# Up projection in Strassen-Winograd form: where the low parts of two halo columns are multiplied

## The chip, the cores and the metric

The kernel runs on one core of a Trainium2 chip (one of the eight; the others are idle). The metric is the device time of one execution in microseconds. Times are medians of several executions of the same program; a profiled execution gives the trace.

## The reference, cut to what matters

One layer of a hybrid decoder: a mixer (attention and a convolution module) with a residual layer norm, and a convolutional feed-forward part. Only the latter is touched here:

```python
h = layer_norm(DEEPNORM_ALPHA * h + mixed @ w_out, ln1_g, ln1_b)   # (1, 1040, 1024) float32
up = causal_dwconv(h @ ffn_w_up, ffn_dw, ffn_dw_b)                 # ffn_w_up (1024, 5632), 3 taps over the sequence
u, g = jnp.split(up, 2, axis=-1)
f = (jax.nn.gelu(g, approximate=False) * u) @ ffn_w_down           # ffn_w_down (2816, 1024)
return layer_norm(DEEPNORM_ALPHA * h + f, ln2_g, ln2_b)
```

The result is float32. The causal convolution over three positions needs, for each half of the sequence (512 positions), the two positions ahead of it: the halo, so 514 columns in all.

## The kernel before, in words

**Three products for one.** TensorE works on a reduced float32 type (`R`, float32r). To keep float32's precision each operand x is split into a high part (its copy in `R`, by ScalarE) and a low part (x minus the high part, by VectorE), and a product is the sum of three matmuls in one accumulation: high x high, high x low, low x high.

**The up projection** (lines 1446 to 1582) is a two by two block product with seven sub-products (Strassen-Winograd): the sequence is one block index (two halves), the 1024 input features the other of the right operand, and a turn `c` (22 of them) makes the 128 channels of the u half and of the gate half that belong together. Its seven right operands B11, B21, BT2, BT4, BT1, BT3, B22 are formed once (`form_t2` and its like, `bsplit`) and stay in SBUF; the seven left operands (weights) are formed and split in each turn by `wsplit`, up to nine ahead of their use. `prod` issues one sub-product: for each of four blocks `k` of 128 features three matmuls. Its columns are cut into two (`SUB`): sub 0 has 258 columns (two of halo and 256), sub 1 has 256. So a sub-product has 24 matmuls, a turn 7 x 24 = 168, and the whole projection 22 x 168 = 3696.

The right operands of sub 0 lie in blocks of `BS[0]` = 260 columns, four high blocks and then four low ones, and the last two columns of a block are unused; those of sub 1 lie in blocks of 256. `bsum(sub, q, hl)` gives the four blocks of the high (`hl` 0) or low part, `bmat` one of them.

**PSUM.** Four tiles of two banks each (`V4, X, Z, Y`, 1024 columns) take the sub-products: sub 0 writes columns 254 to 511, at the end of the first bank, sub 1 columns 512 to 767, at the start of the second, so that one instruction over 514 columns reads both (`at`). Two sub-products accumulate on an earlier one's result in X and one in Y. ScalarE copies X (u13, u2, u13 again) and Y (c22) to SBUF, and VectorE forms the four results c11, c22, c21, c12 of 514 columns (`tt`, line 1542).

**After them** comes `conv_ffn` for each of the four: an activation on ScalarE (line 1461) makes the last tap with the bias, two multiply-adds on VectorE (1462, 1463) the other taps; then gelu on ScalarE (1467), a product on VectorE (1471) and a store to `fd` by SyncE's queue.

**Order of the work.** The instructions of an engine run in the order that a planner gives them when the kernel is built. It goes by priorities (`rank`) and by its own estimate of times; `after` fixes pairs by hand, and `line` chains a row of VectorE instructions, among them the splits of the right operands. Turn 0 has two passes: first sub 1 with all seven products, during which the rest of sub 0's operands is formed (`LATE`, `split_of`), then sub 0. The operands B11 and B21 of sub 0 are formed in two parts, `EARLY` (columns 0 to 129) and `LATE` (130 to 257).

**The down projection** (lines 1588 to 1763) follows. Its first operands are loaded, split and multiplied while the last turn's convolutions still run; it reads `fd`, so its loads stand in SyncE's queue behind the last stores.

Of the kernel before, what the change touches and what calls it, by code (L numbers as in the profile page):

```python
# [25 lines left out]
AF = mybir.ActivationFunctionType  # L26
OP = mybir.AluOpType
# [31 lines left out]

HW = 514  # L60
SUB = [(0, 258), (258, HW)]

WS = 144

BS = [260, 256]
# [47 lines left out]
def tile_hybrid_layer(  # L113
# [3 lines left out]
    nc = tc.nc  # L117
# [12 lines left out]
    def f32(ap):  # L130
        return ap.bitcast(F)
# [24 lines left out]
    FA = arena.tile([P, 6144], F, name="FA")  # L156
# [23 lines left out]
    start = ExitStack()  # L180
# [345 lines left out]
    first = [weights([P, KC, P], in_cols(m)) for m in (4, 5, 0)]  # L526
# [163 lines left out]
    bias = ap.tile([P, NH, 272], F, name="bias")  # L690
# [49 lines left out]
    ins = load(vd, dram(v1d, 0, [[0, P], [J_LEN, NH], [1, J_LEN]]))  # L740
# [17 lines left out]
    for g in range(NKV):  # L758
# [3 lines left out]
        for lo in (0, 64):  # L762
            for o, i in ((Kx[g][lo:, :, 16:144], kr[lo:, 16:T].rearrange("p (n c) -> p n c", c=P)),
                         (Kx[g][lo:, :, 0:16], kr[lo:, 0:16].unsqueeze(1).to_broadcast([P - lo, NB, 16]))):
                if lo == 0:
                    ins = nc.vector.tensor_copy(o, i)
                else:
                    ins = nc.vector.tensor_tensor(o, i, f32(o), OP.subtract)
# [8 lines left out]
    src = ps[:64, :P].rearrange("p (g d) -> p g d", d=HD)  # L777
    nc.scalar.copy(vm[:64, :, 0], src)
    nc.vector.tensor_tensor(vm[:64, :, 1], src, f32(vm[:64, :, 0]), OP.subtract)
    for q4 in range(2):  # L780
# [4 lines left out]
        src = ps[:, :].rearrange("p (n g d) -> p n g d", g=2, d=HD)  # L785
        for g in range(NKV):
            hi, lo = (V[:, q4 * 4:q4 * 4 + 4, g, i] for i in range(2))
# [22 lines left out]
    for h in range(NH):  # L810
        g, r = divmod(h, 4)
        o = ps[:2, h * 16:(h + 1) * 16]
        ins = nc.tensor.matmul(o, q0[g][0][:, r, 0:2], Kx[g][:, 0, 0:16], start=True, stop=False)
# [66 lines left out]
    for i in range(NB):  # L880
# [5 lines left out]
        for g in range(NKV):  # L886
            qh, ql = load_q(g, i) if i else (t[:, :, 2:] for t in q0[g])
            s = ap.tile([P, 4, 272], F, name="s", tag="s", bufs=3)
# [189 lines left out]
    RT = OB[:, 0:2048]  # L1078
# [118 lines left out]
    def bsum(sub, q, hl):  # L1197
        n, s = SUB[sub][1] - SUB[sub][0], BS[sub]
        t, o = B_AT[sub][q]
        return t[:, o + hl * 4 * s:o + (hl + 1) * 4 * s].rearrange("p (k n) -> p k n", k=4)[:, :, :n]  # L1200

    def bmat(sub, q, hl, k):
        return bsum(sub, q, hl)[:, k]

    lined, high = [], []

    def line(ins):

        if lined:
            after(ins, lined[-1])  # L1210
        lined.append(ins)
        return ins
# [3 lines left out]
    def wide(x):  # L1216
        return x.rearrange("p (k n) -> p k n", k=4)
# [3 lines left out]

    def bsplit(sub, q, src, cs=slice(None)):
        with rank(RK_SUMS):
            hi, lo = (bsum(sub, q, hl)[:, :, cs] for hl in range(2))
            src = wide(src)[:, :, cs]
            ins = nc.scalar.copy(hi, src)
            if (sub, q) in ((0, BT2), (0, BT4), (0, BT1), (0, BT3)):
                if high:
                    after(ins, high[-1])
                high.append(ins)  # L1230
            line(nc.vector.tensor_tensor(lo, src, f32(hi), OP.subtract))

    def bsub(out, x, y, cs=slice(None)):
        with rank(RK_SUMS):
# [216 lines left out]
    def ftmp():  # L1451
        i = ft_next[0] % 8
        ft_next[0] += 1
        return FA[:, i * 512:(i + 1) * 512]

    c11, c21, u2 = (FA[:, 4128 + i * HW:4128 + (i + 1) * HW] for i in range(3))
    c12, c22, u13 = (RT[:, i * HW:(i + 1) * HW] for i in range(3))

    def conv_ffn(cc, o):
        t = ftmp()  # L1460
        nc.scalar.activation(t, cc[:, 2:HW], AF.Identity, bias=ffw(3, o), scale=ffw(2, o))  # L1461
        nc.vector.scalar_tensor_tensor(t, cc[:, 1:HW - 1], ffw(1, o), t, OP.mult, OP.add)
        nc.vector.scalar_tensor_tensor(t, cc[:, 0:HW - 2], ffw(0, o), t, OP.mult, OP.add)
        return t
# [47 lines left out]
    for c in range(FC):  # L1512
        V4, X, Z, Y = (pup.tile([P, 1024], F, name=n, tag=n) for n in ("pw", "px", "pz", "py"))
        passes = ((1,), (0,)) if c == 0 else ((0, 1),)
        for subs in passes:
            last = subs == passes[-1]
            w_next = iter(range(7))
            a, b = SUB[subs[0]][0], SUB[subs[-1]][1]

            def at(t):  # L1520
                return t[:, 254 + a:254 + b]

            def prod(q, bank, first):
                if last:
                    w_ahead(9)
                    ah, al = w_ready.pop(0)
                else:
                    ah, al = w_ready[next(w_next)]
                for sub in subs:
                    o = bank[:, 254 + SUB[sub][0]:254 + SUB[sub][1]]  # L1530
                    for k in range(4):
                        ks = slice(k * P, (k + 1) * P)
                        for j, (x, hl) in enumerate(((ah, 0), (ah, 1), (al, 0))):
                            ins = nc.tensor.matmul(o, x[:, ks], bmat(sub, q, hl, k), start=first and k + j == 0,  # L1534
                                                   stop=k == 3 and j == 2, skip_group_check=not first)
                            if k + j == 0 and last_mm:
                                after(ins, last_mm[-1])
                    last_mm.append(ins)

            def tt(*x):  # L1540
                with rank(RK_CHAIN):
                    return nc.vector.tensor_tensor(*x)  # L1542

            def copy(*x):
                with rank(RK_CHAIN):
                    copied.append(nc.scalar.copy(*x))  # L1546

            prod(B11, X, True)
            copy(u13[:, a:b], at(X))
            prod(B21, Z, True)  # L1550
            if last and c not in (0, FH + 1):
                sums_load(c - 1 if c <= FH else c - 2)
            tt(c11[:, a:b], at(Z), u13[:, a:b], OP.add)
            prod(BT2, X, False)
            copy(u2[:, a:b], at(X))
            if not last:
                turn(5, *last_rows, (V4, Z), last_mm, True)
                for q in (B11, B21):
                    split_of(0, q, LATE)
                form_t2(0, LATE)  # L1560
                formed.append(lined[-1])
                form_t4(0, LATE)
                form_t3(0, LATE)
                for q in (BT2, BT4, BT1, BT3, B22):
                    split_of(0, q)
            if last:
                g0 = gelu(conv_ffn(c11, FC + c))
            prod(BT4, V4, True)
            prod(BT1, Y, True)
            copy(c22[:, a:b], at(Y))  # L1570
            prod(BT3, X, False)
            copy(u13[:, a:b], at(X))
            ins = tt(c22[:, a:b], c22[:, a:b], u13[:, a:b], OP.add)
            if last and c not in (0, FH + 1):
                sums_form(c - 1 if c <= FH else c - 2, ins)
            tt(c21[:, a:b], u13[:, a:b], at(V4), OP.subtract)
            prod(B22, Y, False)
            tt(c12[:, a:b], at(Y), u2[:, a:b], OP.add)
            if last:
                f1 = conv_ffn(c22, c)  # L1580
                f_out(c, 0, g0, conv_ffn(c21, c))
                f_out(c, 1, gelu(conv_ffn(c12, FC + c)), f1)
# [234 lines left out]
```

## Time and profile before

| | |
|---|---|
| median of 3 runs | 1271.38 us (1269.64 to 1272.08) |
| the profiled execution | 1271.08 us, span 1269.3 us |
| mean granted clock of TensorE | 0.995 |
| up projection, turn 0 | 609.00 to 633.85 us of the span |
| up projection, turns 1 to 21 | 633.85 to 1047.40 us |
| down projection and the end | 1047.40 to 1269.3 us |

The profile shows one execution. A page gives the busy time of each engine, the span in slices, the chain of work that ended last, and groups of equal instructions. PE is TensorE, DVE VectorE, ACT ScalarE, SP SyncE. In the timeline each row is one instruction or several equal ones in a row (x12): start, time until the last one ends, engine, source line, operation, `out<-in` by the program's names, tile shape. Matmuls overlap, so the time of one says little; the distance of two rows' starts, divided by the count, says how fast they follow each other.

### The profile page before, as it was taken

The numbers are of one execution on the slowest core, as the hardware profiler recorded it, in microseconds if no ns is written. First come the engines' busy times: TensorE is split into PE (matmuls) and PEld (weight loads), VectorE is DVE, ScalarE is ACT, GpSimd is POOL, SyncE is SP. The second block draws the span as 40 slices with busy tenths as digits, with TensorE's granted clock in tenths as the row PEclk, the third lists the DMA queues.
The fourth block names the chain that finished last, engine by engine and source line by source line (L and its number), as shares of the span: only waits on it lengthen the run. The fifth ranks groups of instructions, "written<-read, shape, count | busy, mean of one in ns | idle before, by whom it ended". The sixth has DMA issues, their size and how long they took to land.

```text
span 1269.3 us, 23031 instructions
## 1 busy us (share of the span) xinstructions
PE 1252.8 (99%) x9186; PEld 1184.5 (93%) x9186; DVE 1073.1 (85%) x1854; ACT 591.6 (47%) x1095; POOL 8.1 (1%) x9
## 2 busy tenths in 40 slices
PE   8999999999999999999999999999999999999997
PEld 7999999999999999788899999999999997788886
DVE  7888999999978577548999999998989975987697
ACT  7532355655473223335655455555554553535330
POOL 0000000001000000000000000000000000000000
PEclk9999999999999999999999999999999999999999
DMA  6375643332438364222245546454454566989712
GB/s 252 105 250 149 176 112 96 105 92 83 125 85 226 106 177 125 83 85 82 67 158 198 193 170 212 160 207 150 159 191 170 197 239 242 394 280 369 266 67 83
DMA packets 98701, 212.19 MB, mean 167 GB/s; under 512 B 11411, under 2 KB 38611, under 8 KB 98338
## 3 DMA queue, kind: packets, MB, share of 16 engines
q1 hardware_dynamic: 84474, 199.64, 47.3%
q10 hardware_dynamic: 14120, 11.08, 2.8%
q8 instruction: 72, 1.18, 0.4%
q14 instruction: 35, 0.29, 0.1%
HBM read 150.29 MB, written 62.70 MB: 168 GB/s over the span
## 4 chain that ended last, share of the span: by engine, by line
PE 93%; DVE 2%; DMA 2%; ACT 2%; issue 1%; SPq 0%; DVEq 0%; ACTq 0%
PE px L1534 14%; PE py L1534 10%; PE ps_x L1663 9%; PE ps_z L338 8%; PE ps_z L342 8%; PE ps_z L341 8%; PE pw L1534 5%; PE pz L1534 5%; PE ps_z L1663 5%; PE ps_p L342 2%; PE ps_p L338 2%; PE ps_p L341 2%; PE ps_w L342 2%; PE ps_w L338 2%; PE ps_w L341 2%; PE ps_z L556 2%
## 5 line engine op out<-in xcount | busy, mean ns | idle before, releaser
L342 PE MATMUL ps_z<-RHC,w 128*128 128x256 f32 (+2 forms) x864 | 244.6, 283 | 0.0
L338 PE MATMUL ps_z<-RHO,w 128*128 128x256 f32 (+2 forms) x864 | 244.4, 283 | 0.2 <-ACT FA L734 0.2
L341 PE MATMUL ps_z<-RHO,w 128*128 128x256 f32 (+2 forms) x864 | 243.2, 282 | 0.0
L338 PEld LDWEIGHTS ps_z<-RHO,w 128*128 128x128 f32 x864 | 162.6, 188 | 2.0 <-ACT FA L705 0.7
L341 PEld LDWEIGHTS ps_z<-RHO,w 128*128 128x128 f32 x864 | 162.7, 188 | 0.7
L342 PEld LDWEIGHTS ps_z<-RHC,w 128*128 128x128 f32 x864 | 162.7, 188 | 0.4
L725 DVE SCALAR_TENSOR_TENSOR FA<-cin,cdw,FA 128x1026 f32<-128x1026 f32 x120 | 152.3, 1279 | 0.7
L1356 DVE TENSOR_TENSOR RHO<-wr,RHO 128x512 fp32r<-128x512 f32 x94 | 63.5, 683 | 8.3 <-ACT RHO L1355 8.3
L1355 ACT CAST RHO<-wr 128x512 fp32r<-128x512 f32 x94 | 56.6, 619 | 23.2 <-DVE wr L1373 11.3
L300 ACT CAST w<-wr 128x1024 fp32r<-128x1024 f32 x37 | 38.7, 1046 | 60.8 <-PE ps_z L342 44.8
L734 ACT ACTIVATE FA<-ps_z,colr 128x258 f32<-128x258 f32 (+1 forms) x64 | 30.1, 472 | 69.8 <-PE ps_z L342 57.3
L1373 DVE TENSOR_TENSOR wr<-wr 128x512 f32<-128x512 f32 x88 | 60.0, 682 | 0.1
L303 DVE TENSOR_TENSOR w<-wr,w 128x1024 fp32r<-128x1024 f32 x37 | 45.0, 1217 | 16.3 <-ACT w L300 16.1
L1546 ACT COPY FA<-px 128x514 f32<-128x514 f32 (+2 forms) x23 | 13.1, 571 | 76.7 <-PE px L1534 76.7
L1356 DVE TENSOR_TENSOR w<-wr,w 128x512 fp32r<-128x512 f32 x60 | 40.6, 684 | 4.8 <-ACT w L1355 4.7
L1534 PE MATMUL px<-OA,RHO 128*128 128x258 f32 x324 | 43.2, 283 | 0.0
L1461 ACT ACTIVATE FA<-OB,coll 128x512 f32<-128x512 f32 x44 | 35.9, 815 | 15.0 <-DVE OB L1542 15.0
L1546 ACT COPY OB<-px 128x514 f32<-128x514 f32 (+2 forms) x46 | 26.2, 569 | 34.7 <-PE px L1534 34.5
L1534 PE MATMUL px<-RHC,RHO 128*128 128x258 f32 (+1 forms) x312 | 41.1, 281 | 0.4 <-ACT OB L1546 0.4
L1534 PE MATMUL px<-OC,RHO 128*128 128x256 f32 x324 | 41.5, 277 | 0.0
L1355 ACT CAST w<-wr 128x512 fp32r<-128x512 f32 x60 | 36.3, 618 | 11.1 <-DVE wr L1373 5.1
L1534 PEld LDWEIGHTS px<-OA,RHO 128*128 128x128 f32 x324 | 40.5, 189 | 0.2 <-ACT OB L1546 0.2
(442 smaller groups left out, 3297.2 us busy)
## 6 DMA issues: line engine op xcount, KB each, us to landing
wr<-in_w_up_dram SPq DMA_DIRECT2D x44, 512.0 KB, 3.6
wr<-in_w_z_dram SPq DMA_DIRECT2D x29, 512.0 KB, 3.7
fd<-FA SPq DMA_DIRECT2D x44, 256.0 KB, 2.1
OB<-in_w_down_dram SPq DMA_DIRECT2D x21, 512.0 KB, 4.8
FA<-sd SPq DMA_DIRECT2D x15, 512.0 KB, 9.0
qt<-qd SPq DMA_DIRECT2D x28, 256.0 KB, 4.1
sgd<-FA ACTq DMA_DIRECT2D x48, 128.0 KB, 2.7
td<-OB SPq DMA_DIRECT2D x12, 512.0 KB, 2.7
```

What stands on the lines that cost most here:

```text
L300: ins = nc.scalar.copy(hi, raw)
L303: return nc.vector.tensor_tensor(lo, raw, f32(hi), OP.subtract)
L338: ins = nc.tensor.matmul(ps, al, bh, start=i == 0, stop=False)
L341: nc.tensor.matmul(ps, ah, bh, start=False, stop=False)
L342: last = nc.tensor.matmul(ps, ah, bl, start=False, stop=i == n - 1)
L725: nc.vector.scalar_tensor_tensor(acc[c], cin[:, j:j + U], wc, acc[c], OP.mult, OP.add)
L1355: nc.scalar.copy(hi, src)
L1356: ins = nc.vector.tensor_tensor(lo, src, f32(hi), OP.subtract)
L1373: ins = nc.vector.tensor_tensor(*x)
L1534: ins = nc.tensor.matmul(o, x[:, ks], bmat(sub, q, hl, k), start=first and k + j == 0, stop=k == 3 and j == 2, skip_group_check=not first)
L1546: copied.append(nc.scalar.copy(*x))
L1663: nc.tensor.matmul(banks[i], l[:, ts], r[:, ws], start=first and a and x + k == 0, stop=z and x == len(ops) - 1 and k == 2, skip_group_che ...
```

## The change

In sub 0 the three matmuls of each `k` get different widths. The two halo columns of the low part are stored just before the high part, in columns 0 and 1 of each 260-column block (the high part moves to columns 2 to 259), and the low block keeps only its 256 other columns. Then:

- high weights x [halo low | high], 260 columns, into PSUM columns 252 to 511;
- high weights x low, 256 columns, into 256 to 511;
- low weights x high, 258 columns, into 254 to 511.

The halo's low product so lands in its own two PSUM columns, 252 and 253, beside the halo's other two products in 254 and 255. All copies and sums after it are 516 columns wide and carry both. In `conv_ffn` two activations on ScalarE, of one column each, add column 0 to column 2 and column 1 to column 3. When an operand is split, the halo's low part is a second, small subtraction on VectorE (seven in all, once per operand). Sub 1 is as before, and so are all other stages.

```diff
+CU = HW + 2
...
     def bsum(sub, q, hl):
         n, s = SUB[sub][1] - SUB[sub][0], BS[sub]
         t, o = B_AT[sub][q]
-        return t[:, o + hl * 4 * s:o + (hl + 1) * 4 * s].rearrange("p (k n) -> p k n", k=4)[:, :, :n]
-
-    def bmat(sub, q, hl, k):
-        return bsum(sub, q, hl)[:, k]
+        x = 2 if sub == 0 and hl == 0 else 0
+        v = t[:, o + hl * 4 * s:o + (hl + 1) * 4 * s].rearrange("p (k n) -> p k n", k=4)
+        return v[:, :, x:x + (256 if hl else n)]
+
+    def halo_low(q):
+        t, o = B_AT[0][q]
+        return t[:, o:o + 4 * BS[0]].rearrange("p (k n) -> p k n", k=4)[:, :, 0:2]
+
+    def bmat(sub, q, j, k):
+
+        if sub == 0 and j == 0:
+            t, o = B_AT[0][q]
+            return t[:, o + k * BS[0]:o + (k + 1) * BS[0]]
+        return bsum(sub, q, j % 2)[:, k]
...
     def bsplit(sub, q, src, cs=slice(None)):
         with rank(RK_SUMS):
-            hi, lo = (bsum(sub, q, hl)[:, :, cs] for hl in range(2))
             src = wide(src)[:, :, cs]
+            hi = bsum(sub, q, 0)[:, :, cs]
             ins = nc.scalar.copy(hi, src)
...
-            line(nc.vector.tensor_tensor(lo, src, f32(hi), OP.subtract))
+            n = src.shape[2]
+            first = cs.start or 0
+            x = 2 if sub == 0 and first == 0 else 0
+            at = first - 2 if sub == 0 and first else 0
+            lo = bsum(sub, q, 1)[:, :, at:at + n - x]
+            line(nc.vector.tensor_tensor(lo, src[:, :, x:], f32(hi)[:, :, x:], OP.subtract))
+            if x:
+                line(nc.vector.tensor_tensor(halo_low(q), src[:, :, :2], f32(hi)[:, :, :2], OP.subtract))
...
-    c11, c21, u2 = (FA[:, 4128 + i * HW:4128 + (i + 1) * HW] for i in range(3))
-    c12, c22, u13 = (RT[:, i * HW:(i + 1) * HW] for i in range(3))
+    c11, c21, u2 = (FA[:, 4128 + i * CU:4128 + (i + 1) * CU] for i in range(3))
+    c12, c22, u13 = (RT[:, i * CU:(i + 1) * CU] for i in range(3))
 
     def conv_ffn(cc, o):
         t = ftmp()
+        for i in range(2):
+            nc.scalar.activation(cc[:, 2 + i:3 + i], cc[:, 2 + i:3 + i], AF.Identity, bias=cc[:, i:i + 1], scale=1.0)
+        cc = cc[:, 2:]
         nc.scalar.activation(t, cc[:, 2:HW], AF.Identity, bias=ffw(3, o), scale=ffw(2, o))
...
-            a, b = SUB[subs[0]][0], SUB[subs[-1]][1]
+            a, b = SUB[subs[0]][0] + (2 if subs[0] else 0), SUB[subs[-1]][1] + 2
 
             def at(t):
-                return t[:, 254 + a:254 + b]
+                return t[:, 252 + a:252 + b]
...
                 for sub in subs:
-                    o = bank[:, 254 + SUB[sub][0]:254 + SUB[sub][1]]
                     for k in range(4):
                         ks = slice(k * P, (k + 1) * P)
-                        for j, (x, hl) in enumerate(((ah, 0), (ah, 1), (al, 0))):
-                            ins = nc.tensor.matmul(o, x[:, ks], bmat(sub, q, hl, k), start=first and k + j == 0,
+                        for j, x in enumerate((ah, ah, al)):
+                            o = bank[:, 512:768] if sub else bank[:, (252, 256, 254)[j]:512]
+                            ins = nc.tensor.matmul(o, x[:, ks], bmat(sub, q, j, k), start=first and k + j == 0,
                                                    stop=k == 3 and j == 2, skip_group_check=not first)
```

## The prediction

> **What bounds the kernel now.** I read the page's busy times first, then the chain that ended last, then the busy time by stretch over the up projection, and last the timeline of TensorE inside it.
>
> ```profile
> span 1269.3 us, 23031 instructions
> PE 1252.8 (99%) x9186; PEld 1184.5 (93%) x9186; DVE 1073.1 (85%) x1854; ACT 591.6 (47%) x1095; POOL 8.1 (1%) x9
> PE 93%; DVE 2%; DMA 2%; ACT 2%; issue 1%; SPq 0%; DVEq 0%; ACTq 0%
> core 0: us, PE busy (x) PEld busy (x) DVE busy (x) ACT busy (x) POOL busy (x), PEclk, DMA share, GB/s
> 609.00:633.85 24.85, 23.43 (x186) 22.29 (x185) 21.84 (x37) 15.96 (x32) 0.00 (x0) 1.00 0.21 64
> 633.85:1047.40 413.55, 413.55 (x3530) 413.55 (x3529) 376.33 (x602) 218.88 (x359) 0.00 (x0) 1.00 0.52 185
> ```
>
> TensorE holds 93% of the chain. The last line is the up projection from its second turn c=1 to its end: 21 turns, 413.55/21 = 19.69 us each, TensorE never idle, at full granted clock (1.00). VectorE works 376.33/21 = 17.92 us of a turn, ScalarE 10.42 us. So a nanosecond off the step from one matmul to the next is a nanosecond off the end, as long as VectorE's 1.77 us of room in a turn hold. The line above it is turn 0, with its two passes; there TensorE idles 1.42 us in all.
>
> A matmul's own duration (some 280 ns) is latency. What counts is the step from one start to the next, and the timeline gives it, because equal matmuls are merged:
>
> ```profile
> 799.88 1.61 PE L1534 MATMUL pw<-OA,w 128*128 128x258 f32 x12
> 801.33 1.53 PE L1534 MATMUL pw<-RHC,w 128*128 128x256 f32 x12
> 802.69 1.61 PE L1534 MATMUL py<-OA,w 128*128 128x258 f32 x12
> 804.14 1.53 PE L1534 MATMUL py<-OC,w 128*128 128x256 f32 x12
> ...
> 399.79 0.28 PE L338 MATMUL ps_z<-RHO,w 128*128 128x256 f32 x1
> 408.11 0.28 PE L338 MATMUL ps_z<-RHO,w 128*128 128x258 f32 x1
> 410.98 0.28 PE L338 MATMUL ps_z<-RHO,w 128*128 128x256 f32 x1
> ...
> 92.44 0.29 PE L338 MATMUL ps_z<-RHO,w 128*128 128x272 f32 x1
> 95.48 0.28 PE L338 MATMUL ps_z<-RHO,w 128*128 128x256 f32 x1
> ```
>
> In the up projection twelve matmuls of 258 columns take 801.33 - 799.88 = 1.45 us, 120.8 ns each; twelve of 256 take 802.69 - 801.33 = 1.36 us, 113.3 ns each. Two columns cost 7.5 ns, where the columns themselves are worth little: the next rows say how little. In the z stage three groups of 24 matmuls of 256 run from 399.79 to 408.11 (115.5 ns each), one group of 24 of 258 from there to 410.98 (119.6 ns), and 24 of 272 from 92.44 to 95.48 (126.7 ns). From 258 to 272 a column costs (126.7 - 119.6)/14 = 0.51 ns. So there is a fixed extra of some 4 to 7 ns that a matmul pays once it has more than 256 columns.
>
> **The matmuls.** Of the first half of the columns (sub 0) each k of each product issues three matmuls of 258. After the change they have 260, 256 and 258. The columns are 774 before and after; the number of matmuls and of weight loads is unchanged. But one of three falls to 256. There are 22 turns x 7 products x 4 k = 616 such triples; both passes of turn 0 together make one turn's worth.
> - Before: 3 x 120.8 = 362.4 ns.
> - 260 columns: 120.8 + 2 x 0.51 = 121.8 ns. Upper bound: a further step like that from 256 to 258, 128.3 ns.
> - 256 columns: 113.3 ns is the up projection's own figure, where each block starts a whole multiple of 256 columns after the last; 115.5 ns is the z stage's, whose blocks are 1040 columns apart. The new ones lie 260 columns apart, like neither; nothing tells which is nearer, and I take the middle, 114.4 ns.
> - 258 columns: their operand now starts two columns (8 bytes) later. The z stage's 258 start 8 bytes past a multiple of 16 too (at column U0 = 14 of their blocks, 56 bytes), and run at 119.6; the up projection's at 120.8. I keep 120.8, with 119.6 as the low end.
>
> Sum 121.8 + 114.4 + 120.8 = 357.0 ns, 5.4 ns less; 616 x 5.4 = 3.3 us. Low end of the triple: 121.8 + 113.3 + 119.6 = 354.7, a gain of 4.7 us. High end: 128.3 + 115.5 + 120.8 = 364.6, a loss of 1.4 us.
>
> The Trainium skill, TensorE: Matmul & The Clock Gate, section "Back-to-back issue gap", speaks against this change: it gives a step of N/2.4 + 2.5 ns, so that only the sum of columns counts, and three matmuls of 774 columns in all would take 330.0 ns both ways, a gain of nothing. The trace disagrees: by that rule 256 to 258 is 0.8 ns, and the rows above have 7.5 and 4.1.
>
> **ScalarE.** Each of the four conv_ffn of a turn gets two more activations of one column, 176 in all.
>
> ```profile
> L270 ACT ACTIVATE sd<-mv,eps 128x1 f32<-128x1 f32 x16 | 4.6, 294 | 44.5 <-DVE mv L265 44.5
> L909 ACT ACTIVATE sm<-sm 128x4 f32<-128x4 f32 x16 | 3.2, 199 | 0.5 <-DVE OB L857 0.4
> ACT FA L1546 <- PE px L1534: 71.9, 19, 5.0
> ACT OB L1546 <- PE px L1534: 30.7, 31, 2.6
> ACT OB L1546 <- PE py L1534: 23.6, 19, 3.3
> DVE FA L1462 <- ACT FA L1461: 0.3, 1, 0.3
> ```
>
> The nearest rows are 294 ns (one column, bias from a tile, as here) and 199 ns (four columns). The two are independent of each other, so a pair is between 0.4 and 0.6 us: 1.6 to 2.4 us a turn on top of 10.4, of 19.7. I cost this at nothing, and these lines name the cover. They are the waits of 19 turns: ScalarE stood waiting for TensorE before its copies out of PSUM (L1546), 3.8 us before the u2 copy, 1.0 and 1.2 us before the others. The adds eat into that idle time. If it is gone, a copy is late, and queued behind the adds are the copies that free banks X and Y; but the next write to the same bank comes one product later (24 matmuls, 2.81 us), so TensorE waits only when a copy is more than 2.8 us late. VectorE's first multiply (L1462) follows the ScalarE activation L1461 and waited for it once, 0.3 us: it gets there late by itself, and the adds come before L1461. Its room of 1.77 us a turn is the second cover. The two columns more in each copy and sum are worth a few ns a turn.
>
> **VectorE before turn 1.** Seven splits of sub 0 each get a second small subtraction (4 x 2 elements), in the fixed order that the next splits also stand in. Five of them lie between the two passes, where TensorE follows closely:
>
> ```profile
> 613.11 0.16 DVE L272 SCALAR_TENSOR_TENSOR sd<-sd 128x1 f32<-128x1 f32 x1
> 613.30 0.16 DVE L273 SCALAR_TENSOR_TENSOR sd<-sd 128x1 f32<-128x1 f32 x1
> 628.79 1.23 DVE L1231 TENSOR_TENSOR OA<-FA,OA 128x1032 fp32r<-128x1032 f32 x1
> 629.93 1.23 DVE L1231 TENSOR_TENSOR RX<-FA,RX 128x1032 fp32r<-128x1032 f32 x1
> 630.96 1.59 PE L1534 MATMUL px<-OA,w 128*128 128x258 f32 x12
> 632.39 1.62 PE L1534 MATMUL py<-RX,w 128*128 128x258 f32 x12
> ```
>
> A small operation steps 0.19 us here (613.30 - 613.11). The split of BT3 ends at 630.02 and TensorE uses it at 630.96: 0.94 us of room, against four small ones (BT2, BT4, BT1, BT3), 0.76 us. B22 ends at 631.16 and is used at 632.39: 1.23 us against 0.95. So they are just covered; I cost them at 0.1 us, between 0 and 0.5.
>
> **The change of stage.** After the last product TensorE goes on with the first products of the down projection and then stands.
>
> ```profile
> 1064.22 0.69 DVE L1471 TENSOR_TENSOR FA<-FA 128x512 f32<-128x512 f32 x1 [0.70 <-ACT FA L1467]
> 1069.31 0.82 SPq L124 DMA_DIRECT2D OB<-in_w_down_dram  x1
> 1078.61 1.04 ACT L1625 CAST RHO<-OB 128x1024 fp32r<-128x1024 f32 x1 [0.24 <-DMA OB<-in_w_down_dram]
> 1079.71 2.90 PE L1663 MATMUL ps_x<-RHO,RHC 128*128 128x512 f32 x5 [2.15 <-ACT RHO L1625]
> ```
>
> The last gated product (L1471, 1064.22) is stored; SyncE's queue waits for that store and only then issues the load whose weights TensorE needs at 1079.71, after 2.15 us of idling. All of it hangs on the last evacuation, so it moves up with TensorE. In the new program the last conv_ffn's two adds stand ahead of its activation, 0.4 to 0.6 us, in a stretch in which VectorE's queue (sums, splits, products) is full without a break and ScalarE waits for it. I cost it at 0.1 us, between -0.7 (the order of stores in SyncE's queue is a little different) and +1.0.
>
> Sum: 1271.08 (the profiled execution's time, span 1269.3 and 1.8 around it) - 3.3 + 0.1 + 0.1 = 1268.0 us. The median of the runs shown, 1271.38, is 0.3 above this execution; I leave that in the range.
>
> **Rivals.**
> - *Only columns count.* The extra belongs to the place of the operand (blocks 258 or 260 columns apart, odd starts), not to the count above 256; the new 256s lie in the same places and keep 120.8 less their two columns, 119.8, and 260 has 121.8. Triple 362.4, no gain; with the small costs 1271.3 us. For it: the z stage's 256 are 2.2 ns slower than the up projection's at the same count, so place matters. Against: in the z stage 256 and 258 lie in the same blocks, and 4.1 ns stand between them, not 1.0.
> - *VectorE becomes the bound* (slower). The adds stand between VectorE's sum and the activation that VectorE waits for. If VectorE has to wait them out each time, 0.5 us at four places, a turn is 17.92 + 2.0 = 19.92 us on VectorE against 19.54 on TensorE and 19.69 now: 21 x 0.23 = 4.8 us slower, 1275.9 us. It decides from 0.44 us per place (1.77/4). Against: a single such wait of 0.3 us in 19 turns, and other work stands between.
> - *260 pays a second step* (128.3 ns): 616 x 2.2 = 1.4 us lost, 1272.7 us. Against: 272 columns run at 126.7.
>
> **How the numbers follow.** Chances: forecast 0.68, only columns 0.17, VectorE bound 0.08, second step 0.04, other 0.03. A measurement of this kernel tells some 0.2% (2.5 us) from no change. Of the forecast's own spread (1265.6 with the triple's low end and the stage change's, to 1269.9 with 256 at 115.5 and the small costs' high ends) about 0.06 lies within that bound of no change. So faster 0.62, same 0.25 (that 0.06, the columns rival, the second step's low half), slower 0.13. The range is from 1265.6, the forecast's low end, to 1271.9: the columns rival's 1271.3, the 0.3 by which the median lies above this execution, and 0.3 of the small costs' bounds. It leaves out the two slower cases.
>
> **What would show it.** In the changed kernel's timeline the runs of twelve in sub 0 should step 119.0 ns on average, and those of sub 1 still 113.3; a turn should be 7 x 4 x 5.4 = 0.15 us shorter, 19.54 us, with TensorE busy all through. The durations of 128x260 and 128x258 should look alike and that of 128x256 shorter. ScalarE should be some 2 us a turn busier, its waits for px and py shorter, and TensorE should wait for none of it. Wrong: a turn of 19.7 (only columns), a turn set by VectorE with waits of L1462 for L1461 in each, or a longer stand before the first ps_x product than 2.15 us.

## The result, and the profile after

The changed kernel takes 1273.29 us (median of 17 runs, 1271.36 to 1276.06), the kernel before 1270.93 us beside it (17 runs, 1268.56 to 1272.08): ratio 1.0019 [1.0012, 1.0026], the brackets being the 95% interval. It is 0.19% slower where 0.24% faster was forecast. The profiled execution of the changed kernel took 1271.61 us.

The page after: span, busy times, and the chain's shares by engine.

```profile
span 1269.8 us, 23206 instructions
PE 1254.2 (99%) x9186; PEld 1186.5 (93%) x9186; DVE 1075.3 (85%) x1861; ACT 620.8 (49%) x1271; POOL 8.1 (1%) x9
PE 91%; DVE 4%; DMA 2%; ACT 2%; issue 1%; SPq 0%; DVEq 0%; ACTq 0%
```

ScalarE has 176 instructions and 29.2 us more, TensorE has as many matmuls as before. The busy times over turns 1 to 21 of the up projection, with its bounds in this execution (columns as in the prediction's view):

```profile
632.59:1049.46 416.87, 416.87 (x3530) 416.87 (x3529) 378.11 (x602) 247.47 (x530) 0.00 (x0) 1.00 0.52 183
```

Turns 1 to 21 take 416.87 us where they took 413.55: 19.85 us a turn instead of 19.69 (19.54 was forecast). TensorE is still busy all through at the full granted clock, so it waits for nobody: its matmuls themselves follow one another more slowly. The timeline says which (products BT4, BT1 and BT3 of one turn):

```profile
799.92 1.60 PE L1555 MATMUL pw<-OA,w 128*128 128x260 f32 x12
801.36 1.57 PE L1555 MATMUL pw<-RHC,w 128*128 128x256 f32 x12
802.77 1.59 PE L1555 MATMUL py<-OA,w 128*128 128x260 f32 x12
804.20 1.58 PE L1555 MATMUL py<-OC,w 128*128 128x256 f32 x12
805.61 1.60 PE L1555 MATMUL px<-OA,RHO 128*128 128x260 f32 x12
807.05 1.54 PE L1555 MATMUL px<-RHC,RHO 128*128 128x256 f32 x12
808.43 1.60 PE L1555 MATMUL py<-RX,RHO 128*128 128x260 f32 x12
```

The prediction's rows show BT4 and BT1 in the kernel before; its BT3 follows them there:

```profile
805.50 1.60 PE L1534 MATMUL px<-OA,RHO 128*128 128x258 f32 x12
806.94 1.54 PE L1534 MATMUL px<-RHC,RHO 128*128 128x256 f32 x12
808.32 1.61 PE L1534 MATMUL py<-RX,RHO 128*128 128x258 f32 x12
```

The rows named 128x260 are the runs of twelve of sub 0 (260, 256 and 258 columns), those named 128x256 the runs of sub 1. Sub 0 takes 801.36 - 799.92 = 1.44, then 1.43 and 1.44 us; before it was 1.45, 1.45 and 1.44. Sub 1, of which the change touches neither shape nor operand nor place, takes 802.77 - 801.36 = 1.41 us in the first two products shown (117.5 ns a matmul) and 1.38 in the third; before it was 1.36 in the first two and 1.38 in the third. In the changed kernel five of a turn's seven products (B11, B21, BT4, BT1, B22) run sub 1 like the first two, at a steady 117 or 118 ns from one start to the next; BT2 and BT3 settle at 113, as before. Per turn, sub 0 went from 10.12 us (seven runs, mean of turns 1 to 21) to 10.04, sub 1 from 9.58 to 9.81. Times 21: 1.6 us won, 4.9 us lost, 3.3 us in all, which is 416.87 - 413.55.

The rest of the profiled executions differs by 609.48 against 610.68 in the start of the up projection, ahead of the first matmul that the change touches (the kernels below start it between 609.0 and 611.6), and by 1.6 us less after it, nearly all of it at the change of stage:

```profile
1081.18 0.73 PE L1684 MATMUL ps_x<-RHO,RHC 128*128 128x512 f32 x2 [1.55 <-ACT RHO L1646]
1082.44 1.89 PE L1684 MATMUL ps_x<-RHO,RHC 128*128 128x512 f32 x7 [0.53 <-DVE RHO L1647]
```

TensorE stands 1.55 us instead of 2.15, then 0.53 us once more; its next seven matmuls take 1.89 us, where the first five after the stand took 2.90 before. Two executions of one kernel, e7 and e11 below, differ by as much in the same place (after its second stand each runs 22 of these matmuls, in 6.88 and in 5.29 us), so the 1.6 us are no more than scatter between executions.

**What the trace of before already had.** In the first pass of turn 0 sub 1 runs alone. The timeline of the kernel before shows there:

```profile
610.68 1.58 PE L1534 MATMUL px<-OC,RHO 128*128 128x256 f32 x12
612.10 1.58 PE L1534 MATMUL pz<-OC,RHO 128*128 128x256 f32 x12
...
618.60 1.52 PE L1534 MATMUL py<-OC,w 128*128 128x256 f32 x12
619.96 1.52 PE L1534 MATMUL px<-RHC,w 128*128 128x256 f32 x12
```

The first run takes 612.10 - 610.68 = 1.42 us, the one at 618.60 takes 1.36. The same run of matmuls has two steady steps, some 117.7 and 113.3 ns, and the profile of before showed both. The durations tell them apart too: 1.57 or 1.58 against 1.52 to 1.54.

### The profile page after: what moved, and what is told of

The parts are those of the page before. It is cut to its first block, busy times and chain, and to the rows that moved or that the text cites. A ratio compares the mean times of both kernels' runs of the same rounds, so it can differ in the third digit from the quotient of the medians.

```text
span 1269.8 us, 23206 instructions
## 1 busy us (share of the span) xinstructions
PE 1254.2 (99%) x9186; PEld 1186.5 (93%) x9186; DVE 1075.3 (85%) x1861; ACT 620.8 (49%) x1271; POOL 8.1 (1%) x9
## 4 chain that ended last, share of the span: by engine, by line
PE 91%; DVE 4%; DMA 2%; ACT 2%; issue 1%; SPq 0%; DVEq 0%; ACTq 0%
PE px L1555 15%; PE py L1555 9%; PE ps_x L1684 9%; PE ps_z L339 8%; PE ps_z L343 8%; PE ps_z L342 8%; PE pz L1555 5%; PE pw L1555 5%; PE ps_z L1684 5%; PE ps_p L343 2%; PE ps_p L339 2%; PE ps_p L342 2%; PE ps_w L343 2%; PE ps_w L339 2%; PE ps_w L342 2%; PE ps_z L557 2%
## 5 line engine op out<-in xcount | busy, mean ns | idle before, releaser
L1567 ACT COPY FA<-px 128x516 f32<-128x516 f32 (+2 forms) x23 | 13.1, 569 | 71.8 <-PE px L1555 71.8
L1555 PE MATMUL px<-OA,RHO 128*128 128x260 f32 x324 | 43.4, 283 | 0.0
L1555 PE MATMUL px<-RHC,RHO 128*128 128x256 f32 (+2 forms) x312 | 40.8, 280 | 0.4 <-ACT OB L1567 0.4
L1555 PEld LDWEIGHTS px<-OC,RHO 128*128 128x128 f32 x324 | 39.8, 188 | 0.1
L1555 PEld LDWEIGHTS px<-RHC,RHO 128*128 128x128 f32 x312 | 38.4, 188 | 0.6 <-ACT OB L1567 0.6
```

Of the source, the lines that this page charges most:

```text
L1555: ins = nc.tensor.matmul(o, x[:, ks], bmat(sub, q, j, k), start=first and k + j == 0, stop=k == 3 and j == 2, skip_group_check=not first)
```

## The experiments

Times are medians, ratios are to the kernel before on the same chip. "Settled" means that the last half of a run of twelve keeps one step, the short one (113 to 114 ns) or the long one (117 to 118). A run whose steps keep changing throughout is said to wander. Times of sub 0 and sub 1 are a turn's seven runs from start to start, mean of turns 1 to 21. e13, e15 and e16 stand in the text alone.

| kernel | sub 0, us | sub 1, us | turn, us | sub 1 at the long step, of 147 | ratio |
|---|---|---|---|---|---|
| before | 10.12 | 9.58 | 19.70 | 1 | |
| after | 10.04 | 9.81 | 19.85 | 105 | 1.0019 [1.0012, 1.0026] |
| e1, no adds | 10.04 | 9.81 | 19.85 | 105 | 1.0024 [1.0014, 1.0035] |
| e2, order 260, 258, 256 | 10.02 | 9.75 | 19.77 | 74 | 0.9999 [0.9989, 1.0008] |
| e3, high part 2 later, 258 | 10.15 | 9.72 | 19.87 | 63 | 1.0018 [1.0008, 1.0027] |
| e4, low 256 in old place | 10.10 | 9.60 | 19.70 | 0 | 0.9993 [0.9984, 1.0002] |
| e5, eleven of twelve 256 | 10.08 | 9.69 | 19.77 | 0 | 1.0011 [1.0000, 1.0022] |
| e6, last k 258, 256, 260 | 10.05 | 9.81 | 19.87 | 105 | 1.0016 [1.0006, 1.0026] |
| e7, last k 260, 258, 256 | 10.06 | 9.60 | 19.67 | 5 | 0.9989 [0.9979, 0.9999] |
| e8, both parts 2 later, 258 | 10.09 | 9.69 | 19.78 | 41 | 1.0018 [1.0009, 1.0028] |
| e9, blocks 256 apart, 256 | 9.92 | 9.74 | 19.66 | 63 | 0.9980 [0.9971, 0.9989] |
| e10, blocks 256 apart, 258 | 10.03 | 9.74 | 19.77 | 63 | 1.0014 [1.0005, 1.0023] |
| e11, e7 again | 10.06 | 9.60 | 19.66 | 2 | 0.9992 [0.9983, 1.0000] |
| e12, e7 with low blocks 256 apart | 10.01 | 9.75 | 19.77 | 74 | 0.9997 [0.9988, 1.0006] |
| e14, sub 1 first | 10.12 | 9.58 | 19.69 | 0 | 0.9993 [0.9983, 1.0004] |
| e17, e9 8 columns later | 9.76 | 9.74 | 19.50 | 83 | 0.9959 [0.9945, 0.9973] |
| e18, all starts 32 past 64 | 10.02 | 9.87 | 19.89 | 126 | 1.0038 [1.0024, 1.0052] |

A run of twelve that passes from one step to the other in its last half counts as neither.

### Is it ScalarE? (e1)

```diff
-        for i in range(2):
-            nc.scalar.activation(cc[:, 2 + i:3 + i], cc[:, 2 + i:3 + i], AF.Identity, bias=cc[:, i:i + 1], scale=1.0)
```

> The changed kernel without the 176 one-column activations of conv_ffn; the halo's low part is left out of the result. Theory A (the matmuls of sub 1 settle at one of two steps, 113 or 118 ns, and the run of sub 0 before them decides which): TensorE's stream is the same, so a turn stays at 19.85 us and sub 1 at 118 ns in five products and 113 in two. Theory B (ScalarE's extra work slows TensorE's reads): sub 1 is back at 113 ns in all seven, a turn at 19.6 us, about 1268 us.

1274.39 us, and the same five of seven products at the long step, as in these two of its rows:

```profile
793.94 1.58 PE L1553 MATMUL px<-OC,RHO 128*128 128x256 f32 x12
795.35 1.59 PE L1553 MATMUL pz<-RHO,w 128*128 128x260 f32 x12
```

795.35 - 793.94 = 1.41 us. The adds cost nothing that can be measured, and taking them away gives nothing back.

### Which part of the matmuls' change? (e2 to e5, e8)

e2, the changed kernel with another order of the three in each k:

```diff
-                        for j, x in enumerate((ah, ah, al)):
+                        for i, (j, x) in enumerate(((0, ah), (2, al), (1, ah))):
```

> The changed kernel with the three matmuls of a k in the order 260, 258, 256. Sub 1 is untouched. Theory A: another end of sub 0's run, so other products of sub 1 at 113 or 118 ns than in the changed kernel; a turn anywhere between 19.55 us (all at 113) and 19.95 (all at 118). Theory C (the new layout as such slows what follows it): five products at 118, two at 113, a turn of 19.85 us.

1270.89 us. The instructions are the same, only their order is not, and sub 1 takes the long step in 74 twelves instead of 105. Which products take it changes from turn to turn: those that have the short step in one turn have the long one in the next.

e3, the kernel before with the high parts two columns later in their blocks, all widths 258:

```diff
-        return t[:, o + hl * 4 * s:o + (hl + 1) * 4 * s].rearrange("p (k n) -> p k n", k=4)[:, :, :n]
+        x = 2 if sub == 0 and hl == 0 else 0
+        return t[:, o + hl * 4 * s:o + (hl + 1) * 4 * s].rearrange("p (k n) -> p k n", k=4)[:, :, x:x + n]
```

> The kernel before, with nothing changed but the place of sub 0's high parts: two columns (8 bytes) later, all three matmuls of 258 columns, into the old PSUM columns. Theory A: the starts of the operands belong to what sets the end of the run, so sub 1 may settle at 118 ns in some products; at most 21 x 7 x 12 x 4.3 ns = 7.6 us slower. Rival (only the mix of widths does it): sub 1 at 113 ns in all seven, a turn at 19.70 us, 1271 us.

1273.08 us: a move of 8 bytes with every width as before costs what the whole change costs. Sub 1 has its two steps side by side:

```profile
794.12 1.52 PE L1535 MATMUL px<-OC,RHO 128*128 128x256 f32 x12
795.48 1.61 PE L1535 MATMUL pz<-RHO,w 128*128 128x258 f32 x12
796.93 1.58 PE L1535 MATMUL pz<-OC,w 128*128 128x256 f32 x12
798.34 1.62 PE L1535 MATMUL px<-OA,w 128*128 128x258 f32 x12
```

1.36 us in B11, 798.34 - 796.93 = 1.41 us in B21.

e4, the kernel before with the low matmul 256 wide in its old place:

```diff
+                            y = 2 if sub == 0 and hl == 1 else 0
+                            ins = nc.tensor.matmul(o[:, y:], x[:, ks], bmat(sub, q, hl, k)[:, y:], ...
```

> The kernel before, with sub 0's high x low matmul cut to 256 columns (its two halo columns are left out of the result), everything in its old place. The prediction's price: the middle matmul falls from 120.8 to 114.4 ns, a turn 28 x 6.4 ns = 0.18 us shorter, 19.51 us. If a matmul of 256 among wider ones gains nothing (as the profile of the changed kernel suggests), sub 0 stays at 119 to 121 ns. Sub 1: theory A allows either step.

1270.11 us. Sub 1 keeps the short step in all 147 twelves. Sub 0 gains 0.02 us a turn as a mean (0.03 in the typical turn), not the 0.18 that a step of 113.3 would give.

e5, the same for all but the first of the twelve:

> The kernel before with sub 0 at 256 columns in eleven of the twelve matmuls of a sub-product (the first keeps 258; the halo's other eleven are left out of the result), all in their old places. If the count decides: runs of 256 in sub 0 settle at 113 or 118 ns like those of sub 1, so a turn is 7 x 24 x 113.3 = 19.04 us plus up to 0.7 for the slower step, some 1257 to 1271 us. If the place decides (blocks 260 columns apart): sub 0 stays at 119 to 121 ns and the turn at 19.6 to 19.7 us.

1271.9 us. Eleven of twelve matmuls have 256 columns and sub 0 still runs at 10.08/84 = 120 ns. The two columns are worth (10.12 - 10.08)/77 = 0.5 ns each time, not 7.5. Sub 1 settles at the short step in all 147 runs, and yet takes 9.69 us a turn instead of 9.58: its first five steps are 118.2 ns on average, where before they were 115.0. So the run ahead also sets how soon a run settles, and not only at which step.

e8, the kernel before with all of sub 0 8 bytes later (RX 8 earlier):

> The kernel before with all of sub 0's operands, high and low, two columns (8 bytes) later (in the last one two earlier), 258 columns throughout. If the start of an operand decides by itself: another set of products of sub 1 at 118 ns than none, a turn above 19.70 us. If only the distance between the high and the low parts matters (moved against each other in the run with the high parts alone shifted): as before, all seven at 113 ns, 19.70 us.

1272.8 us. Sub 1 takes the long step in two products, and sub 0 gains a little. Again only places differ.

### The last matmuls ahead of sub 1 (e6, e7, e11)

e6 and e7, the changed kernel with another order in the last k alone (e6 `trio[::-1]`):

```diff
+                        trio = ((0, ah), (1, ah), (2, al))
+                        for i, (j, x) in enumerate(trio if k < 3 or sub else (trio[0], trio[2], trio[1])):
```

> The changed kernel, in sub 0 the fourth k in the order 258, 256, 260; all else as changed. Theory A (the end of sub 0's run decides at which step sub 1 settles): the set of products at 118 ns changes, a turn between 19.55 and 19.95 us. Theory C (the layout as such): 19.85 us, five products at 118 ns.

> The changed kernel, in sub 0 the fourth k in the order 260, 258, 256; all else as changed. Theory A: again another set of products of sub 1 at 118 ns; with all seven at 113 it would be 19.61 us a turn, some 2 us below the kernel before. Theory C: 19.85 us, five products at 118 ns.

> The changed kernel with 260, 258, 256 columns in the last k of a product and 260, 256, 258 in the other three, once more and in more rounds. If the order of the last three matmuls sets what step the next run of sub 1 settles in: sub 1 at 113 ns in all seven products, turn 19.66 us, ratio 0.999 to the kernel before, 1269.4 us. If the earlier result was chance: 118 ns in some of them, up to 1273 us.

e6 takes 1272.68 us with the long step in other products than in the changed kernel, but again in five. e7 takes 1269.36 us, again 1269.80 us in e11 (11 runs, before 1271.15): five and two of 147 at the long step.

```profile
792.23 1.53 PE L1556 MATMUL px<-OC,RHO 128*128 128x256 f32 x12
793.60 1.60 PE L1556 MATMUL pz<-RHO,w 128*128 128x260 f32 x12
795.04 1.53 PE L1556 MATMUL pz<-OC,w 128*128 128x256 f32 x12
796.41 1.59 PE L1556 MATMUL px<-OA,w 128*128 128x260 f32 x12
```

Sub 1 is back at 1.37 us. One swap in the last of four triples of a product takes the whole loss away: it is not in the work, but in what the run of sub 1 comes after.

### Columns or blocks? (e9, e10)

e9 lays sub 0 as sub 1 is laid:

```diff
+        return t[:, o + hl * 1024:o + (hl + 1) * 1024].rearrange("p (k n) -> p k n", k=4)
...
+                            n = 258 if sub == 0 and k + j == 0 else 256
```

> The kernel before, with the operands of sub 0 laid as those of sub 1 are: blocks 256 columns apart, each matmul 256 wide (the first of a product 258, so that its bank is begun whole). The halo columns' contributions are left out. Place theory (what holds sub 0 near 120 ns a step is that its blocks lie 260 columns apart): a run of twelve in sub 0 falls from 1.45 us to 1.36 (113.3 ns) or 1.41 (117.7 ns), the two steps that sub 1 shows; at 1.36 the turn is 7 x 0.085 = 0.6 us shorter, 19.1 us, and the time some 13 us less, 1258 us; at 1.41 it is 0.25 us shorter, some 1266 us. Stream theory (the step belongs to the sequence of matmuls and weight loads, not to the blocks): sub 0 stays at 1.43 to 1.45 us as it did with eleven of twelve matmuls 256 wide in the old blocks, 1271 us.

e10 has 258 there again but for the last low block:

> The same blocks 256 columns apart, but sub 0's matmuls 258 wide again (the last low block 256 wide); the two extra columns of each are read from the next block, so the values of two columns are not the product's. Count theory (a matmul pays a fixed extra of some 7 ns once it has more than 256 columns): twelve take 1.44 to 1.45 us, the time stays at 1271 us whatever the run of 256 columns does. Place theory: twelve take only the columns more, 12 x 2 x 0.42 to 0.51 ns = 0.01 us over the run with 256 columns, that is 1.37 or 1.42 us, 1260 or 1267 us.

1267.93 and 1272.76 us. Product BT2 of sub 0 in e9, then in e10:

```profile
796.10 1.57 PE L1541 MATMUL px<-OA,w 128*128 128x258 f32 x12
797.50 1.54 PE L1541 MATMUL px<-OC,w 128*128 128x256 f32 x12
```

```profile
797.44 1.60 PE L1541 MATMUL px<-OA,w 128*128 128x258 f32 x12
798.88 1.53 PE L1541 MATMUL px<-OC,w 128*128 128x256 f32 x12
```

1.40 and 1.44 us. Both theories fall in the form given. e10 by itself is near what the count theory expected (1.43 us, for 1.44 to 1.45), but with 256 columns e9 comes out hardly shorter. The ten matmuls of a run that differ cost (10.03 - 9.92)/70 = 1.6 ns for two columns, so there is no extra of 7 ns above 256 columns in these runs. But at 256 columns, 256 apart, sub 0 doesn't settle either: its steps wander between 112 and 125 ns, 118 on average.

### State carried along, or places? (e12, e13)

e12 is e7 with the low blocks 256 columns apart.

> As the kernel of the run before it in this list, but the low parts of sub 0, which are 256 columns wide in the changed kernel, lie 256 columns apart rather than 260 (the whole reference is computed). Place theory: the four of twelve matmuls that read them step some 113 to 115 ns rather than 119 to 120, a run of twelve in sub 0 falls from 1.440 us to 1.415, 22 x 7 x 0.025 = 3.9 us, 1265.5 us. If the step is that of the whole run and one operand in three is not enough: sub 0 stays at 1.44 us and the time at 1269.4 us. If sub 1 settles at 118 ns in some products for it, each costs 0.05 us a turn, 1.1 us in all, up to 7.7 us: 1277 us.

1270.69 us. Sub 0 gains 0.05 us a turn and sub 1 loses 0.15, because it now takes the short and the long step by turns, through all products and on into the next turn. A turn has seven products, so each product has the short step in one turn and the long one in the next. e13 is e12 with one product issued twice:

```diff
-                for sub in subs:
+                for sub in (subs * 2 if c == 11 and q == B11 else subs):
```

> The kernel of the run before (low blocks 256 columns apart), with the first product of turn 11 issued twice, the second time over the first (the whole reference is computed, 24 matmuls more, 2.8 us). In the run before, the products of sub 1 settle by turns at 113 and at 118 ns: in even turns 113 118 113 118 113 118 113, in odd turns 118 113 118 113 118 113 118. State theory (which of the two steps a run takes follows from the one before it in TensorE's queue): one product more turns the pattern over, and from turn 12 on the even turns show 118 113 118 113 118 113 118. Place theory (the place of the weights, which moves on by seven products a turn, sets the step): nothing changes after turn 11, since the weights lie where they lay; even turns show 113 118 113 118 113 118 113. Time 1273.5 us either way.

1273.28 us in a single run. The same two products (B11 and B21, weights in the same tile `w`, turn 12) in e12, then in e13:

```profile
851.00 1.54 PE L1558 MATMUL px<-OC,w 128*128 128x256 f32 x12
852.37 1.58 PE L1558 MATMUL pz<-RHO,w 128*128 128x260 f32 x12
853.79 1.58 PE L1558 MATMUL pz<-OC,w 128*128 128x256 f32 x12
855.21 1.61 PE L1558 MATMUL px<-OA,w 128*128 128x260 f32 x12
```

```profile
855.04 1.58 PE L1558 MATMUL px<-OC,w 128*128 128x256 f32 x12
856.45 1.61 PE L1558 MATMUL pz<-RHO,w 128*128 128x260 f32 x12
857.89 1.54 PE L1558 MATMUL pz<-OC,w 128*128 128x256 f32 x12
859.27 1.59 PE L1558 MATMUL px<-OA,w 128*128 128x260 f32 x12
```

1.37 and 1.42 us in e12, 1.41 and 1.38 in e13. Up to turn 11 the two kernels agree run by run; from the doubled product on, sub 1 has the short step where it had the long one, and the long where it had the short, in 69 of the 70 products of the remaining ten turns (the other counts as neither in e12). Instructions, operands and places are the same. So which step a run settles in follows from what the queue had before it, and it is handed on from run to run.

### What keeps sub 0 from settling? (e14 to e18)

e14 is the kernel before with sub 1 ahead of sub 0 (`for sub in subs[::-1]`); e15 is e9 with the operand of sub 1 read in both runs (`bmat(1, q, hl, k, n)`); e16 is e9 with the halves of the PSUM tile exchanged.

> The kernel before with the two halves of the columns in the other order: in each product from turn 1 on the run of twelve of sub 1 comes first, that of sub 0 (258 columns) second (the whole reference is computed). Order theory (the run that comes first with new weights doesn't settle, the second does): sub 1 takes some 1.42 us, unsettled at about 119 ns, and sub 0 settles at 114 to 115 or 118 to 119 ns, 1.37 to 1.43 us. Operand theory (sub 0's tile or its half of the bank sets it): sub 0 stays at 1.43 to 1.45 us unsettled, sub 1 at 1.36 or 1.41. Time 1266 to 1275 us under the first, 1271 to 1277 us under the second.

> The kernel with sub 0's blocks 256 columns apart and 256 columns a matmul, in which the first run of twelve of a product now reads the operand of sub 1 as the second does (sub 0's columns are left out, the halo's too). Operand theory: the first run settles as the second does, 1.36 or 1.41 us, the turn falls from 19.66 to between 19.1 and 19.5 us, 1256 to 1264 us. Order theory, and that of the bank's half: the first run stays unsettled at 1.40 to 1.43 us, 1268 us.

> The kernel with sub 0's blocks 256 columns apart, in which from turn 1 on sub 0 writes the upper half of the bank pair and sub 1 the lower (the halo is left out, and the halves of the output's columns are taken for each other). Theory of the bank's half: the run of sub 0 settles at 113 or 118 ns and that of sub 1 doesn't. Order and operand theories: sub 0 stays unsettled at 1.40 to 1.43 us, sub 1 at 1.36 or 1.41; 1268 us.

e14, 1270.05 us: sub 1, now first, keeps the short step, and sub 0 its 120 ns.

```profile
793.57 1.53 PE L1534 MATMUL pz<-OC,w 128*128 128x256 f32 x12
794.93 1.61 PE L1534 MATMUL pz<-RHO,w 128*128 128x258 f32 x12
```

e15, 1265.72 us (ratio 0.9954 [0.9938, 0.9970]): with sub 1's operand the first run settles as well, at the step that the second then has; a product of 24 takes 791.81 - 789.07 = 2.74 us or 2.82.

```profile
789.07 2.90 PE L1541 MATMUL px<-OC,RHO 128*128 128x258 f32 x24
791.81 2.99 PE L1541 MATMUL pz<-OC,w 128*128 128x258 f32 x24
794.63 2.90 PE L1541 MATMUL px<-OC,w 128*128 128x258 f32 x24
```

e16, 1266.44 us in a single run: in the other half of the bank pair sub 0 still wanders (112 to 120 ns), and sub 1, in sub 0's half, settles, at 113 ns in all 147 runs.

So it is sub 0's operand. By the addresses in the built programs, which no trace here holds, every block of sub 1 begins 32 bytes past a multiple of 128, those of sub 0 in e9 at a multiple of 128, and those in the kernels before and after at another place in each block. The source bears out the difference where both lie in one tile: in `RHC` sub 0 begins at column 40 and the blocks of sub 1 at column 112 past a multiple of 256 columns, 72 columns or 288 bytes further, which is 32 past a multiple of 128. e17 is e9 with sub 0 moved 8 columns, 32 bytes, on:

```diff
+        o += 0 if sub else 8
```

> The kernel with sub 0's blocks 256 columns apart and 256 columns a matmul (the halo left out), with all of sub 0's blocks moved 8 columns (32 bytes) further on. As before the move they begin at whole multiples of 128 bytes, where sub 1's blocks begin 32 bytes past such a multiple; after it both do. Start theory (what keeps a run from settling is where its blocks begin within 64 or 128 bytes): the run of sub 0 settles as that of sub 1 does, at 113 or 118 ns, 1.36 to 1.41 us rather than 1.40 to 1.43, the turn falls from 19.66 to between 19.1 and 19.5 us, 1256 to 1264 us. If it is another property of sub 0's tiles: sub 0 stays unsettled at 1.40 to 1.43 us and the time near 1268 us.

1266.28 us. Sub 0 (258 in the name) and sub 1 of B21, then sub 0 of BT2:

```profile
793.46 1.54 PE L1542 MATMUL pz<-RHO,w 128*128 128x258 f32 x12
794.84 1.52 PE L1542 MATMUL pz<-OC,w 128*128 128x256 f32 x12
796.20 1.53 PE L1542 MATMUL px<-OA,w 128*128 128x258 f32 x12
797.57 1.58 PE L1542 MATMUL px<-OC,w 128*128 128x256 f32 x12
```

1.38 us and 1.37 us in sub 0 where e9 had 1.42 and 1.40. All runs of sub 0 now settle, 84 of 147 at the short step. The start of the blocks decided whether they settle. The time is above the 1256 to 1264 us expected, as e15's is: 146 of the 294 runs of both halves still settle at the long step, some 0.05 us each. e18 carries it to the whole computation: 260, 256, 260 columns, with every block of sub 0 beginning 32 bytes past a multiple of 64 (by turns 32 and 96 past one of 128).

> The changed kernel with every block of sub 0 beginning 32 bytes past a multiple of 64, as sub 1's do (the whole reference is computed): the low parts 256 columns apart, the high parts with the halo's low parts before them 272 columns apart, and the third matmul of a triple 260 wide too, so that it begins where the first does: 260, 256, 260. Start theory: sub 0 settles, at 113 ns with some 0.5 ns for each column above 256, 12 x 113.3 + 8 x 4 x 0.5 = 1.375 us a run of twelve, or at 118 ns, 1.43 us; the changed kernel has 1.43 to 1.44. With sub 1 between 1.36 and 1.41 as it falls, the turn is 19.2 to 19.7 us, the time 1261 to 1270 us. If starts within 64 bytes are not enough (it is 128, or the distance of 272): sub 0 stays at 1.43 to 1.45 us unsettled, 1270 to 1274 us.

1275.88 us, the longest of all and above both times expected, with sub 1 at the long step in 126 of 147.

```profile
799.39 1.60 PE L1557 MATMUL px<-OA,w 128*128 128x260 f32 x12
800.83 1.58 PE L1557 MATMUL px<-OC,w 128*128 128x256 f32 x12
```

Sub 0 stays at 1.43 to 1.44 us and wanders. A start within 64 bytes is not enough, or a run with two widths, or one wider than 256 columns, doesn't settle; these were not told apart.

## Why the prediction was wrong, point by point

- **The step that failed: sub 1 "still 113.3".** The sum priced 616 triples of sub 0 and left sub 1 out, as untouched. Sub 1 has two steady steps for the same instructions, and the stream ahead of it sets which one (e13, e2, e7). Before, nearly all its runs sat at the short one; after, five of seven products at the long one, some 50 ns a run, 4.9 us over turns 1 to 21. Without most of that loss the change has a small gain: e7 and e11 are the same work with another order in one triple of four, and their medians are 1.3 us below the kernel before.
- **The triple was mis-sized.** Sub 0 won (10.119 - 10.043) us over 28 triples, 2.7 ns a triple instead of 5.4: 1.6 us over turns 1 to 21. The term that failed is 256 columns at 114.4 ns, the middle of the steps of sub 1 and of the z stage. e4 and e5 show that a 256-column matmul among sub 0's blocks costs about what one of 258 does, less 0.5 to 1 ns, and e10 against e9 that there is no jump at 256 there. Of the difference between sub 0 and sub 1, on which the price rested, the width is the smallest part: a turn of sub 0 goes from 10.12 us to 10.08 with eleven of twelve matmuls narrowed (e5), to 9.92 with the blocks 256 apart (e9) and to 9.76 with their start moved by 32 bytes (e17, 84 of 147 runs at the short step). Sub 1 had 9.58, with nearly all its runs at the short step.
- **The rival "only columns count"** was right that the extra belongs mostly to the operand's place. It forecast no gain in sub 0 and no change in sub 1, so it missed the loss as well. What the prediction held against it, the 4.1 ns between 256 and 258 columns in the z stage, is in good part a matter of settling, as this row of the kernel before shows:

```profile
401.21 0.28 PE L338 MATMUL ps_z<-RHO,w 128*128 128x256 f32 x1
```

  The 72 matmuls of 256 columns that begin at 399.79 take (401.21 - 399.79)/12 = 118.3 ns each at first, and (408.11 - 401.21)/60 = 115.0 after that; those of 258 keep wandering, at 119.6. So the width may still decide whether a run settles: no run of 258 columns was tried at a start that settles.

  The Trainium skill, TensorE: Matmul & The Clock Gate, section "Back-to-back issue gap", was set aside in the prediction because the trace disagreed. By its formula, an estimate, two columns are worth 0.8 ns; e5 has 0.5 and e10 against e9 1.6, so on that point it was nearer than the reading of the rows. The section gives this formula for an isolated matmul, and some 131 ns at 512 columns for a stream with a weight load before each, as here. The stream of this trace is nearer to the formula, which gives an estimate of 215.8 ns at 512: in the down projection of the kernel before, 24 matmuls of 512 columns take 1116.96 - 1111.52 = 5.44 us, 226.7 ns each. The section has one step for one width, and the runs show two.
- **260 columns** show no jump: the change's runs of sub 0 are shorter on average, not longer, than before.
- **ScalarE** was costed right. Its busy time in turns 1 to 21 rose by (247.47 - 218.88)/21 = 1.4 us a turn, a little less than the 1.6 to 2.4 expected. The waits of the same 19 turns, after:

```profile
ACT FA L1567 <- PE px L1555: 67.7, 17, 4.7
ACT OB L1567 <- PE py L1555: 25.3, 19, 3.5
DVE FA L1483 <- ACT FA L1482: 0.7, 2, 0.4
```

  and one group of the adds in the groups by line:

```profile
L1480 ACT ACTIVATE OB<-OB 128x1 f32<-128x1 f32 x88 | 21.1, 287 | 12.8 <-DVE OB L1563 12.8
```

  An add takes 287 ns on average, where the nearest row of before had 294. ScalarE still waits for TensorE before its copies, VectorE waited for the activation 0.7 us in all, and TensorE for neither. The rival "VectorE becomes the bound" has nothing for it, as e1 shows.
- **VectorE before turn 1** and **the change of stage** were small, as costed: turn 0 takes 632.59 - 609.48 = 23.11 us against 633.85 - 610.68 = 23.17, and the two stands together are 1.55 + 0.53 = 2.08 us where one of 2.15 was. The 1.5 us by which the stage's first matmuls ran faster is no more than the scatter told of above.

The profiled executions differ by 0.5 us and the medians by 2.4. The trace's 3.3 us in the up projection is the part that repeats in every turn.

## What to carry to other kernels

Before a step from one matmul to the next is read as the price of a shape, look whether the same shape has another step elsewhere in the trace: a short first pass may show it. In a stream without pauses, an edit to one run of matmuls can move the step of the runs behind it, so those belong in the sum as a term with two values (here 1.36 and 1.41 us a run), and a different order of the same matmuls (e7, 0.9989 and 0.9992 of before) is a cheap thing to try. Try it over several runs, because a gain of 0.1% is no more than the width of the interval.

## What the runs showed of the hardware

- A run of equal matmuls of 256 columns with a weight load before each settles at 113.3 or at 117.7 ns a matmul, at the same granted clock (1.00 in turns 1 to 21), and the choice is inherited from the runs before (e13: one product more turned over all that followed). What in the engine carries it was not found.
- Runs of 256 columns whose blocks begin 32 bytes past a multiple of 128 (addresses as told under e16) settle; at a multiple of 128 they wander, at 118 ns on average (e9) and 117 in the other half of the bank (e16), and 32 bytes further on they settle again (e17). Why that start, which other starts do, and whether it has to do with the weights' own places, stays open; so does what kept e18 from settling.
- Two columns more at the same blocks, 258 instead of 256, cost 0.5 to 1.6 ns a matmul in runs that wander (e4, e5, e9, e10).
